# Im2col on one core: two input loads instead of three, and a first store timed by copies instead of a wait

## The chip, the cores and the metric

The kernel runs on one core of a Trainium2 chip. The metric is the device time of one execution in microseconds (us). The median of the four runs shown is 91.89 us.

## The reference

The input `x` has the shape (16, 64, 32, 32) in float32, the window is 3 x 3. Every window position becomes a column:

```python
cols = np.zeros((batch, c * kernel_size * kernel_size, h_out * w_out), dtype=np.float32)
for i in range(h_out):
    for j in range(w_out):
        patch = x[b, :, i:i + kernel_size, j:j + kernel_size]
        cols[b, :, col_idx] = patch.ravel()
```

With `h_out = w_out = 30`, one image channel (32 x 32) becomes nine planes of 30 x 30 = 900 numbers, one for each offset (ki, kj) in the window. Nothing is calculated. 4.19 MB are read and 33.18 MB are written.

## The kernel before

The 16 x 64 = 1024 channels are spread over the 128 partitions, eight neighbouring channels on each (`CPP = 8`). A partition's input is then 8 x 1024 numbers, 32 KB in one piece; its output is 8 x 9 x 900 numbers, 259.2 KB in one piece.

The whole input stays in SBUF, in `in_tile`. Three loads (L39 to L42) fill it, cut by rows of 32 numbers. The first takes rows 0 to 32, which is channel 0, 4 KB per partition. The second (`bulk`) takes rows 32 to 200, 21 KB. The third takes the rest, 7 KB. All are issued by SP. The end of `tile_im2col_kernel` moves the first load ahead of the program's opening barrier, so that it is issued as the first instruction of the span.

The loop over `c` (L47) takes two channels at a time. Each turn gets an `out_tile` of 2 x 9 planes from a pool of two buffers, so the third turn waits until the first turn's stores have landed, and the fourth until the second's has. A plane is one copy (L55 on ScalarE, ACT; L57 on VectorE, DVE) that reads a shifted 30 x 30 window of the channel and writes 900 numbers in a row. The list `on_act` deals the copies out in a fixed pattern of five, two to ACT and three to DVE. Of channel 0's nine planes ACT gets four and DVE five.

The stores go out on SP too (L60 and L75). In the first turn each channel has a store of its own of 32400 bytes per partition, since it can start earlier; the other three turns store both channels at once, 64800 bytes per partition. The order is written by hand (`manual_schedule`): each engine does its work in program order, and SP issues its DMAs one after the other, each when what it waits for is done. So SP's order is three loads, two stores of one channel, three stores of two channels.

A dependency added by hand (L66) makes the first store wait for the second load as well, though the store does not need its data.

Of the kernel before, what the change touches and what calls it, by code (L numbers as in the profile page):

```python
# [1 line left out]

# [3 lines left out]


def _im2col(ctx, tc, x, K, out):


    nc = tc.nc
    P = nc.NUM_PARTITIONS

    B, C, H, W = x.shape
    HO = H - K + 1
    WO = W - K + 1
    KK = K * K
    assert out.shape == (B, C * KK, HO * WO)
    CPP = B * C // P
    assert CPP * P == B * C and C % CPP == 0 and CPP % 4 == 0  # L20

    x_v = x.rearrange("b (cp c2) h w -> (b cp) (c2 h w)", c2=CPP)
    out_v = out.rearrange("b (cp c2 kk) n -> (b cp) c2 (kk n)", c2=CPP, kk=KK)

    in_pool = ctx.enter_context(tc.tile_pool(name="in_pool", bufs=1))
    out_pool = ctx.enter_context(tc.tile_pool(name="out_pool", bufs=2))

    ctx.enter_context(tc.manual_schedule())

    in_tile = in_pool.tile([P, CPP, H, W], x.dtype, name="in_tile")  # L30
    in_flat = in_tile.rearrange("p c h w -> p (c h w)")

    def load(queue, r0, r1):

        return queue.dma_start(
            out=in_flat[:, r0 * W : r1 * W], in_=x_v[:, r0 * W : r1 * W]
        )

    cuts = [0, H, 200, CPP * H]  # L39
    first = load(nc.sync, cuts[0], cuts[1])  # L40
    bulk = load(nc.sync, cuts[1], cuts[2])
    load(nc.sync, cuts[2], cuts[3])  # L42


    on_act = (False, True, False, True, False)
    n = 0
    for c in range(0, CPP, 2):  # L47
        out_tile = out_pool.tile([P, 2, KK, HO, WO], x.dtype, name="out_tile")
        for s in range(2):
            for kk in range(KK):  # L50
                ki, kj = divmod(kk, K)
                src = in_tile[:, c + s, ki : ki + HO, kj : kj + WO]
                dst = out_tile[:, s, kk]
                if on_act[n % len(on_act)]:
                    nc.scalar.copy(out=dst, in_=src)  # L55
                else:
                    nc.vector.tensor_copy(out=dst, in_=src)  # L57
                n += 1
            if c == 0:
                st = nc.sync.dma_start(  # L60
                    out=out_v[:, s],
                    in_=out_tile[:, s].rearrange("p kk i j -> p (kk i j)"),
                )
                if s == 0:

                    tc.add_manual_dep(  # L66
                        st.ins,
                        bulk.ins.name,
                        mybir.DependencyInfo(
                            mybir.DependencyClass.Sync, mybir.DependencyReason.DATA  # L70
                        ),
                        reason="the store follows the bulk of the loads",
                    )
        if c > 0:
            nc.sync.dma_start(  # L75
                out=out_v[:, c : c + 2].rearrange("p c n -> p (c n)"),
                in_=out_tile.rearrange("p c kk i j -> p (c kk i j)"),
            )
    return first


def kernel(
    tc: tile.TileContext,
    x: bass.AP,
    kernel_size: bass.AP,
    out: bass.AP,
):
    with ExitStack() as ctx:
        first = _im2col(ctx, tc, x, int(kernel_size), out)


    tc.close()
    tc.compile()  # L93
    blocks = tc.nc.main_func.blocks
    load = first.ins
    home = next(b for b in blocks if any(i.name == load.name for i in b.instructions))
    home.instructions = [i for i in home.instructions if i.name != load.name]
    head = list(blocks[0].instructions)
    at = next(
        k  # L100
        for k, i in enumerate(head)
        if i.engine == load.engine and type(i).__name__ == "InstDrain"
    )
    head.insert(at, load)
    blocks[0].instructions = head


# [1 line left out]
_INS = ['x', 'kernel_size']  # L109
_OUTS = [((16, 576, 900), 'float32')]  # L110

_NUMBERS = {'kernel_size': 3}


# [26 lines left out]
```

## Time and profile before

| | before |
|---|---|
| runs shown | 91.76, 91.54, 92.19, 92.02 us |
| median | 91.89 us |
| profiled execution, its time | 92.38 us |
| profiled execution, its span | 90.60 us |
| bytes read and written | 4.19 MB, 33.18 MB |
| copies on DVE | 43, of 625 ns |
| copies on ACT | 29, of 939 ns |
| DMAs, all issued by SP | 3 loads, 5 stores |

The profile is of one execution. The span goes from its first to its last instruction; 1.78 us of its time lie outside. Times in the profile count from the span's start. "SPq" is the sequencer of SP, which only waits and issues DMAs. A DMA "lands" when its semaphore shows at the waiting side that the data is there. The copies overlap a little on their engine, so a row of several copies is shorter than their number times the duration of one.

A DMA over 128 partitions is cut into 128 packets, one for each partition's piece, eight for each of the sixteen DMA engines. The trace holds a record of every packet (start, length, bytes), but not which of the sixteen engines ran it; since an engine's packets follow each other closely, the records can be sorted into sixteen chains.

### The profile page before, as it was taken

What the parts mean: (1) busy time and instruction counts of PE and PEld (TensorE: products, weight loads), DVE (VectorE), ACT (ScalarE), POOL (GpSimd) and SP (SyncE); (2) the same over time, 40 slices, a digit from 0 to 9 for tenths busy, and PEclk for the clock granted to TensorE, in tenths of its full rate; (3) what the DMA queues carried; (4) which work ended last, traced back from release to release, by engine and by line L of the source; (5) the groups of instructions that cost most, each with busy time, mean ns of one, the idle gap of its engine ahead of it and who ended that gap; (6) DMA issues with size and microseconds to landing.
All of it is one profiled execution on the core that took longest, in us unless ns stands there. A gap on an engine that the chain in (4) does not pass through costs nothing.

```text
span 90.6 us, 140 instructions
## 1 busy us (share of the span) xinstructions
DVE 23.5 (26%) x43; ACT 26.2 (29%) x30; POOL 0.2 (0%) x4
## 2 busy tenths in 40 slices
DVE  0380199980000069700000299400000000000000
ACT  5391199950000069930000299400000000000000
POOL 0000000000000000000000000000000000000000
DMA  5999999997999999973999999999999999994690
GB/s 123 460 408 446 373 485 458 458 401 300 458 458 443 672 458 458 458 343 143 458 458 458 458 458 458 458 458 458 458 458 458 429 458 458 458 458 200 286 458 0
DMA packets 1152, 37.37 MB, mean 412 GB/s; under 512 B 128, under 2 KB 128, under 8 KB 384
## 3 DMA queue, kind: packets, MB, share of 16 engines
q1 hardware_dynamic: 1152, 37.37, 96.5%
HBM read 4.19 MB, written 33.18 MB: 412 GB/s over the span
## 4 chain that ended last, share of the span: by engine, by line
DMA 46%; DVE 16%; DVEq 1%; issue 0%; SPq 0%
DMA out_dram<-out_tile 35%; DVE out_tile L57 16%; DMA in_tile<-in_x_dram 11%; DVEq L93 1%; DVEq L57 0%; SPq L75 0%
## 5 line engine op out<-in xcount | busy, mean ns | idle before, releaser
L55 ACT COPY out_tile<-in_tile 128x900 f32<-128x900 f32 x29 | 24.9, 939 | 30.7 <-DMA out_dram<-out_tile 25.3
L57 DVE COPY out_tile<-in_tile 128x900 f32<-128x900 f32 x43 | 23.5, 625 | 34.1 <-DMA out_dram<-out_tile 26.0
L55 ACT ACT_TABLE_LOAD x1 | 1.3, 1283 | 0.8 <-PEq L122 0.8
L122 POOL MEMSET const-bfloat16-1.0<- 128x1 bf16 x1 | 0.1, 101 | 0.0
L122 POOL MEMSET const-uint8-127<- 128x1 uint8 x1 | 0.1, 101 | 0.0
L122 POOL MEMSET const-float32-0.0<- 128x1 f32 x1 | 0.1, 98 | 0.2 <-issue 0.2
L122 POOL MEMSET const-float32-1.0<- 128x1 f32 x1 | 0.1, 98 | 0.0
## 6 DMA issues: line engine op xcount, KB each, us to landing
out_dram<-out_tile SPq DMA_DIRECT2D x3, 8100.0 KB, 31.3
out_dram<-out_tile SPq DMA_DIRECT2D x2, 4050.0 KB, 14.9
in_tile<-in_x_dram SPq DMA_DIRECT2D x1, 2688.0 KB, 10.1
in_tile<-in_x_dram SPq DMA_DIRECT2D x1, 896.0 KB, 11.9
in_tile<-in_x_dram SPq DMA_DIRECT2D x1, 512.0 KB, 3.7
```

The source lines that it names most:

```text
L55: nc.scalar.copy(out=dst, in_=src)
L57: nc.vector.tensor_copy(out=dst, in_=src)
L93: tc.compile()
L122: nc = _bacc.Bacc("TRN2", target_bir_lowering=False, num_devices=1)
```

## The change

The input comes in two loads: rows 0 to 64 (channels 0 and 1, 8 KB per partition) and all the rest (24 KB per partition). The first is the one that is moved ahead of the barrier.

The dependency of the first store on the second load is gone. The store now waits for channel 0's nine copies alone. Six of these (all with `kk % 3 != 1`) are on ACT instead of four, and three on DVE instead of five. All other planes are dealt out as before, so that ACT has 31 copies in all and DVE 41. Stores, tiles and the order on each engine are the same.

```diff
-    cuts = [0, H, 200, CPP * H]
-    first = load(nc.sync, cuts[0], cuts[1])
-    bulk = load(nc.sync, cuts[1], cuts[2])
-    load(nc.sync, cuts[2], cuts[3])
+    first = load(nc.sync, 0, 2 * H)
+    load(nc.sync, 2 * H, CPP * H)
...
-                if on_act[n % len(on_act)]:
+                if kk % 3 != 1 if c + s == 0 else on_act[n % len(on_act)]:
                     nc.scalar.copy(out=dst, in_=src)
...
-                st = nc.sync.dma_start(
+                nc.sync.dma_start(
                     out=out_v[:, s],
                     in_=out_tile[:, s].rearrange("p kk i j -> p (kk i j)"),
                 )
-                if s == 0:
-
-                    tc.add_manual_dep(
-                        st.ins,
-                        bulk.ins.name,
...
-                        reason="the store follows the bulk of the loads",
-                    )
```

More of the change, by code (lines that the diff above doesn't have):

```diff
@@ L63, in _im2col @@
                 )
-                if s == 0:
-                    tc.add_manual_dep(
-                        st.ins,
-                        bulk.ins.name,
-                        mybir.DependencyInfo(
-                            mybir.DependencyClass.Sync, mybir.DependencyReason.DATA
-                        ),
-                        reason="the store follows the bulk of the loads",
-                    )
         if c > 0:
```

## The prediction

> **What bounds the kernel now.** I read the page first: engine shares, the forty slices, the DMA queue.
>
> ```profile
> span 90.6 us, 140 instructions
> ...
> DVE 23.5 (26%) x43; ACT 26.2 (29%) x30; POOL 0.2 (0%) x4
> ...
> DMA  5999999997999999973999999999999999994690
> GB/s 123 460 408 446 373 485 458 458 401 300 458 458 443 672 458 458 458 343 143 458 458 458 458 458 458 458 458 458 458 458 458 429 458 458 458 458 200 286 458 0
> ...
> q1 hardware_dynamic: 1152, 37.37, 96.5%
> ```
>
> Both copying engines are three quarters idle; one DMA queue fills 96.5% of sixteen engines' span. Next the issues and their times to landing, as the DMA view gives them in narrow windows, in issue order (issue times from the timeline: 0.00, 0.80, 1.19, 10.97, 14.30, 20.21, 39.33, 57.71).
>
> ```profile
> in_tile<-in_x_dram SPq DMA_DIRECT2D x1, 512.0 KB, 3.7
> in_tile<-in_x_dram SPq DMA_DIRECT2D x1, 2688.0 KB, 10.1
> in_tile<-in_x_dram SPq DMA_DIRECT2D x1, 896.0 KB, 11.9
> ```
> ```profile
> out_dram<-out_tile SPq DMA_DIRECT2D x1, 4050.0 KB, 11.8
> ```
> ```profile
> out_dram<-out_tile SPq DMA_DIRECT2D x1, 4050.0 KB, 18.1
> ```
> ```profile
> out_dram<-out_tile SPq DMA_DIRECT2D x1, 8100.0 KB, 31.3
> ```
> ```profile
> out_dram<-out_tile SPq DMA_DIRECT2D x1, 8100.0 KB, 32.1
> ```
>
> Issue plus landing gives: last load 13.1, stores 22.8, 32.4, 51.5, 70.6, 89.8 us. The steps between are 9.7, 9.6, 19.1, 19.1 and 19.2 us for stores of 4.15, 4.15 and three times 8.29 MB, so 430 to 434 GB/s throughout. The stores run back to back; the time is 13.1 us of loading, 76.7 us of storing, and 0.8 us to the span's end. Only the first part can change. At the stores' rate 4.19 MB of loads would take 9.7 us, so 3.4 us there is not transfer.
>
> For those 3.4 us I sorted the trace's packet records into sixteen chains, each packet beginning where another ended. First packets start at 1.02 to 1.42 us and take 0.39 to 0.89 us, where later packets of that size take 0.159. Fifteen chains then run without a break and end their loads between 11.40 and 11.89. The sixteenth had finished its share of the first load earliest, at 2.744; its next packet begins 0.68 us later, at 3.425, and lasts 1.51 us where its kind takes 0.80. That chain needs 10.02 us from there to its last load, against about 8.61 for a chain without the stall: 1.41 us lost. It ends its loads at 12.76, and goes on without a gap to 89.29. The other fifteen end at 88.53 to 88.68. So one stalled chain sets this execution's end.
>
> Last, the waits and the timeline around the first store:
>
> ```profile
> SPq L60 <- DMA in_tile<-in_x_dram: 9.3, 1, 9.3
> ```
> ```profile
> 3.69 3.48 ACT L55 COPY out_tile<-in_tile 128x900 f32<-128x900 f32 x4 [1.61 <-DMA in_tile<-in_x_dram]
> 3.69 2.78 DVE L57 COPY out_tile<-in_tile 128x900 f32<-128x900 f32 x5 [3.69 <-DMA in_tile<-in_x_dram]
> 10.90 8.54 ACT L55 COPY out_tile<-in_tile 128x900 f32<-128x900 f32 x10 [3.73 <-DMA in_tile<-in_x_dram]
> 10.90 9.23 DVE L57 COPY out_tile<-in_tile 128x900 f32<-128x900 f32 x17 [4.43 <-DMA in_tile<-in_x_dram]
> 10.97 3.67 SPq L60 DMA_DIRECT2D out_dram<-out_tile  x2
> ```
>
> Channel 0 is copied by 7.17, yet SP holds its store until the second load has landed. Issued at 10.97, its packets begin at 11.83 to 11.96, or 0.86 us after the issue: by then fifteen chains have been empty for 0.01 to 0.57 us. Only the stalled chain loses nothing by it.
>
> **The change, part by part.**
>
> *One load fewer.* A chain's eight packets follow each other every 155.3, 795.4 and 268.3 ns for 4096, 21504 and 7168 bytes: 4.7 ns each plus 0.0368 ns per byte. By that line 8192 bytes take 306 and 24576 take 908. Now 8 x (155.3 + 795.4 + 268.3) = 9.75 us; then 8 x (306 + 908) = 9.71. That is on the path: minus 0.04, minus 0.05 with the semaphore packet that goes. A DMA issue on SP (0.33 to 0.42 us) goes too, at a time when SP only waits.
>
> The Trainium skill, "DMA: Bandwidth & Descriptors", section "Anatomy of one DMA", puts a fixed cost of about 2.0 us on each DMA (fitted on GpSimd's path), which would make this edit worth minus 2.0 us. The row shows 6 ns between one load's last packet and the next load's first.
>
> *The first load twice as large.* It lands later, by 8 x (306 - 155) = 1.21 us: at 3.69 + 1.21 = 4.90. Lower bound 3.69 (nothing added), upper 7.4 (the whole time to landing doubles). I take 4.90, since start-up is paid once per chain and the spacing is measured. DVE and ACT begin 1.2 us later, which only the first store can feel.
>
> *The stall.* What made that chain wait is not in the trace. Its shape is that of a chain that ran dry: the earliest to finish, a gap, then a packet with 0.71 us too much, like the 0.24 to 0.74 us too much of the very first packets. If its part of the second load was ready at 3.42, a first load that lasts until 3.95 or later on every chain (2.744 + 1.21) covers it. Bounds: minus 1.41 us on this chain, or nothing; above nothing if it strikes a chain without this one's lead, which ended its first load 0.57 us ahead of the last. I take the cover, because the packet began late; a slow read alone would have made it long, not late.
>
> *Six planes on ACT, no hold.* Four copies take 3.48 us and ten 8.54, so each further one 0.843; six take 3.48 + 2 x 0.843 = 5.17. DVE's three end long before. Channel 0 is ready at 4.90 + 5.17 = 10.07, SP issues 0.03 later (as after ACT's last copy at 39.30, issued 39.33), at 10.10, and packets are ready 0.86 later, at 10.96. The chains end loading at 11.35 to 11.84 (today's less 0.05). So the store is in time by 0.4 us, the gaps of 0.01 to 0.57 close, and the load packets hide the issue: while the same store was issued at 10.97, load packets kept their 0.272 us. Bounds with landing at 3.69 and 7.4: packets at 9.75, or 13.46, 1.6 us too late for the last chain. Behind the store on SP is the second one, which is ready later anyway.
>
> *What follows.* Channel 1 no longer waits for the second load. ACT does nine copies, 3.48 + 5 x 0.843 = 7.70, to 12.6; the second store is issued then instead of at 14.30, while the first runs until after 21. The next tile needs the 24 KB load, landed at about 12.1 instead of 10.9; ACT's seven copies (6.01 us in the fourth tile) end at 18.6, issue near 18.7 against 20.21, and the queue needs it at 31.1. Nothing there reaches the path; its cover is 12 us of queued stores. After that order and counts are the same.
>
> The Trainium skill's "Perfetto Trace Analysis", section "DMA Optimizations", says that smaller pieces let work start sooner where DMA engines are idle; that speaks against merging the loads. Here the copies' later start is 1.2 us, hidden as shown; by the rule alone it would be plus 1.2.
>
> **The sum, in the profiled execution.** Without a stall the last chain leaves its loads at 11.84, and stores take 76.5 (the stalled chain) to 76.8 us (the others): end 88.3 to 88.6, taken as 88.5, against 89.29, so minus 0.8. Its time of 92.38 (span 90.60, 1.78 around it) becomes 91.6. The median shown, 91.89, is 0.49 lower. If all runs had the full stall they come to 91.1. If the runs differ by the stall, a stall-free one today ends at 88.68, which is 92.38 - 0.61 = 91.77, about that of the two fastest (91.54, 91.76); from those the closed gaps take 0.18 (88.68 to 88.5): 91.4 to 91.6. I take 91.4, between the two readings; this case by itself spans 91.0 to 91.7.
>
> **Rivals.**
>
> *The stall stays as it is.* It may be a slow stretch of memory, met by any second load. Then only 0.05 us goes: 91.84, between 91.5 and 92.2. For it: the runs shown spread by 0.65 us, so it may come and go. Against: the late start.
>
> *The stall strikes a chain without a lead: slower.* Place: the first 24 KB packet of a chain that leaves the first load last. It would end its loads at 11.84 + 1.41 = 13.25 instead of 12.76: plus 0.49 on the profiled time, 92.87; on the median 92.4 if all runs stall today, more if they don't; I put it at 92.6. If the median's 0.49 is a shorter stall, its last chain leaves the loads at 12.27, and this decides from 0.9 us of stall on the last chain (11.84 + 0.9 = 12.27 + 0.46). For it: nothing ties the stall to that chain. Against: it did strike the one that was ahead.
>
> *The store comes too late.* If the first load lands after 5.78, 5.78 + 5.17 + 0.03 + 0.86 = 11.84 and all chains run dry. At the bound of 7.4 stores begin at 13.46 and end at 90.1: plus 0.9, 92.8 by the median. Against: it takes 0.9 us more than the spacing gives.
>
> **How the numbers follow.** The covered stall: 0.55, of which 0.40 beyond 0.5% (below 91.43) and 0.15 within. The unchanged stall: 0.22, of which 0.19 within and 0.03 above 92.35. The worse stall: 0.18, slower. The late store: 0.05, of which 0.02 within. So faster 0.40, same 0.36, slower 0.24; 0.5%, 0.46 us, is about what a measurement of this kernel can tell from no change. The range, 91.0 to 92.4, leaves out some 0.08 below and 0.12 above.
>
> **What would show it.** Right: a first landing near 4.9, the first store issued near 10.1, a 24 KB landing near 12.1, no chain idle between loads and store, the first store landing near 21.8 instead of 22.8, the span near 89.7. Wrong: a load landing at 13 or later (a stall), the first store issued after 10.9, or steps between store landings that are no longer 9.6 and 19.1.

## The result, and the profile after

The changed kernel takes 91.45 us (median of 53 runs, 91.25 to 91.69); the kernel before, beside it, 91.64 us (78 runs, 91.37 to 93.78). The ratio is 0.9971, with a 95% interval of 0.9962 to 0.998. So it is 0.3% faster: clear of chance, but within the 0.5% that the prediction called no change. The forecast time was 91.4, and the result lies inside its range. What changed more than the middle is the upper end: 15 of the 78 runs before lie above 92.0 us, and none of the 53 after above 91.69. The means differ by 0.31 us (91.77 and 91.45), and about half of that is this upper end: the other 63 runs of before have a mean of 91.62.

The page of the changed kernel answers the lines of before: the queue, and the load issues.

```profile
span 89.6 us, 136 instructions
...
DMA  5989899999889999995799999999999998489990
...
q1 hardware_dynamic: 1008, 37.37, 97.2%
...
in_tile<-in_x_dram SPq DMA_DIRECT2D x1, 3072.0 KB, 11.4
in_tile<-in_x_dram SPq DMA_DIRECT2D x1, 1024.0 KB, 4.9
```

The first store's time from issue to landing, from the DMA view between 9.5 and 11 us:

```profile
out_dram<-out_tile SPq DMA_DIRECT2D x1, 4050.0 KB, 11.7
```

Its timeline up to the second store (start, length, engine, line, count; in brackets the idle time before and what ended it):

```profile
4.88 13.60 ACT L54 COPY out_tile<-in_tile 128x900 f32<-128x900 f32 x16 [2.82 <-DMA in_tile<-in_x_dram]
4.88 4.93 DVE L56 COPY out_tile<-in_tile 128x900 f32<-128x900 f32 x9 [4.88 <-DMA in_tile<-in_x_dram]
10.07 2.87 SPq L59 DMA_DIRECT2D out_dram<-out_tile  x2
12.19 6.01 DVE L56 COPY out_tile<-in_tile 128x900 f32<-128x900 f32 x11 [2.37 <-DMA in_tile<-in_x_dram]
```

The first load lands at 4.86 (4.90 was forecast), and the first store is issued at 10.07 (10.10) and lands at 21.8 (21.8). The wait on a load that held SP for 9.3 us is gone; SP now waits for the copies:

```profile
SPq L59 <- ACT out_tile L54: 5.5, 2, 3.4
SPq L59 <- DVE out_tile L56: 5.5, 1, 5.5
```

In the packet records, sorted into sixteen chains as before, the chains end their loads between 11.14 and 11.73 and begin the store within 0.01 us. No chain stalls, and none is empty. Stores end at 88.32, and the span is 89.6 (89.7).

So far everything is as forecast, except for the execution it was compared with. A second and a third trace of the kernel before were taken:

> The kernel before, unchanged, for a second trace. If the stall of one chain is a rare event, this trace shows none: the second load then lands near 10.0 instead of 10.88, the held store is issued near 10.1, its packets come near 11.0, no chain is empty, and the span is near 89.7. If the stall comes every time, it is there again and the span is 90 or more.

Measured: 91.60 us, span 89.8. The timeline of this second trace, and its second and third load:

```profile
3.71 3.47 ACT L55 COPY out_tile<-in_tile 128x900 f32<-128x900 f32 x4 [1.64 <-DMA in_tile<-in_x_dram]
...
10.10 4.32 ACT L55 COPY out_tile<-in_tile 128x900 f32<-128x900 f32 x5 [2.92 <-DMA in_tile<-in_x_dram]
10.10 4.39 DVE L57 COPY out_tile<-in_tile 128x900 f32<-128x900 f32 x8 [3.61 <-DMA in_tile<-in_x_dram]
10.16 3.67 SPq L60 DMA_DIRECT2D out_dram<-out_tile  x2
```
```profile
in_tile<-in_x_dram SPq DMA_DIRECT2D x1, 2688.0 KB, 9.3
in_tile<-in_x_dram SPq DMA_DIRECT2D x1, 896.0 KB, 11.1
```

The second load is seen at 10.10 instead of 10.90, and the held store goes out at 10.16 instead of 10.97, nearly where the changed kernel's does (10.07). Its packets meet the end of the loads (11.38 to 11.89) without a gap.

> The same kernel once more, for a third trace, with the same expectation as the second.

Measured: 91.64 us, span 89.9, store issued at 10.26, again no stall. The execution on which the prediction was built, 92.38 us, was thus one of the minority above 92.0. In the common execution, as these two traces show it, the hold and the six planes put the store at nearly the same place.

### The profile page after: what moved, and what is told of

It is laid out like the page before. It is cut to its first block, busy times and chain, and to the rows that moved or that the text cites. A ratio compares the mean times of both kernels' runs of the same rounds, so it can differ in the third digit from the quotient of the medians.

```text
span 89.6 us, 136 instructions
## 1 busy us (share of the span) xinstructions
DVE 22.4 (25%) x41; ACT 27.7 (31%) x32; POOL 0.2 (0%) x4
## 4 chain that ended last, share of the span: by engine, by line
DMA 41%; ACT 15%; DVE 6%; DVEq 1%; issue 0%
DMA out_dram<-out_tile 36%; ACT out_tile L54 15%; DVE out_tile L56 6%; DMA in_tile<-in_x_dram 5%; DVEq L82 1%; DVEq L56 0%
## 5 line engine op out<-in xcount | busy, mean ns | idle before, releaser
L54 ACT COPY out_tile<-in_tile 128x900 f32<-128x900 f32 x31 | 26.5, 940 | 28.2 <-DMA out_dram<-out_tile 25.4
L56 DVE COPY out_tile<-in_tile 128x900 f32<-128x900 f32 x41 | 22.4, 625 | 34.3 <-DMA out_dram<-out_tile 27.0
## 6 DMA issues: line engine op xcount, KB each, us to landing
in_tile<-in_x_dram SPq DMA_DIRECT2D x1, 3072.0 KB, 11.4
```

## The experiments

Times are medians; beside each stands the median of the kernel before, run together with it. The experiments fall into three such groups, each on another chip (1 to 4; 5 to 8; 9, 10 and the two further traces), and the share of before's runs above 92.0 us differs between them: 3 of 17, 1 of 29, 7 of 17. Comparisons across groups go by the ratios to before or by the traces; where medians are compared directly, the text says so.

**1. The hold taken out, nothing else.**

```diff
-                if s == 0:
-
-                    tc.add_manual_dep(
-                        st.ins,
-                        bulk.ins.name,
...
-                        reason="the store follows the bulk of the loads",
-                    )
```

> The kernel before with the first store's wait on the second load taken out and nothing else. Theory A (a chain that stalls after a short first load sets the slow executions): the loads are unchanged, so the stalls stay, and the time stays that of before within 0.15 us, with single executions still above 92.0 us. Theory B (the held store is what costs): without the hold the store is issued near 7.2 us, no chain runs empty, and the time falls to that of the changed kernel, 0.2 us below before.

Measured: 92.78 us (5 runs) beside 91.62, ratio 1.0115 (1.0086 to 1.0145). Both theories fall: the kernel gets slower by 1.1 us (1.16 by the medians, 1.05 by the ratio). The store is issued early, and the last load lands late:

```profile
7.05 6.67 SPq L60 DMA_DIRECT2D out_dram<-out_tile  x2
```
```profile
in_tile<-in_x_dram SPq DMA_DIRECT2D x1, 896.0 KB, 12.1
```

That load was issued at about 1.2, so it lands at 13.3; in the second trace of before it takes 11.1 from the same issue. In the packet records its 7168-byte packets last 431 ns on average instead of 272. Eight on each chain make 1.27 us.

**2. The changed kernel with the old dealing, so with an early store.**

```diff
-                if kk % 3 != 1 if c + s == 0 else on_act[n % len(on_act)]:
+                if on_act[n % len(on_act)]:
```

> The changed kernel with the old dealing of channel 0 (five planes on DVE, four on ACT), so that its store is issued near 8.4 us instead of 10.07. Theory A: the store only waits in the queue behind the loads, so the time is that of the changed kernel within 0.1 us. Theory C (a store issued early, among the loads, disturbs them, and six planes on ACT are needed to time it): slower than the changed kernel by 0.2 us or more, with load packets longer than their 309 and 912 ns after the issue.

Measured: 92.46 us (6 runs) beside 91.62, ratio 1.008 (1.0051 to 1.0109). The time and the load packets are as theory C has them. The timeline shows the store at 8.35, and the next turn's copies waiting for the 24 KB load until 13.07, where the changed kernel has them at 12.19:

```profile
8.35 2.92 SPq L59 DMA_DIRECT2D out_dram<-out_tile  x2
13.07 1.79 ACT L54 COPY out_tile<-in_tile 128x900 f32<-128x900 f32 x2 [2.21 <-DMA in_tile<-in_x_dram]
13.07 1.17 DVE L56 COPY out_tile<-in_tile 128x900 f32<-128x900 f32 x2 [2.22 <-DMA in_tile<-in_x_dram]
```
```profile
in_tile<-in_x_dram SPq DMA_DIRECT2D x1, 3072.0 KB, 12.3
```

In the records the 24 KB packets that start between 4.3 and 9.2 last 912 ns. Those that start from 9.25 to 10 last 0.13 to 0.23 us longer on average, the last ones, from 10.25, 0.6 to 0.73 us longer. The sum is 0.87 us on each chain.

**3. Loads of 4 and 28 KB.**

```diff
-    first = load(nc.sync, 0, 2 * H)
-    load(nc.sync, 2 * H, CPP * H)
+    first = load(nc.sync, 0, H)
+    load(nc.sync, H, CPP * H)
```

> The changed kernel with loads of 4 and 28 KB per partition. Six planes of channel 0 on ACT, no hold, store issued near 8.9 us. Theory A: the short first load is back, so a chain may run empty before its part of the second load is there; executions above 92.0 us come back, about 2 in 10, and the median is about that of before. Theory D (it is the third load and its extra packets that cost): no such executions, median as the changed kernel's.

Measured: 92.14 us (12 runs) beside 91.62, ratio 1.0063 (1.0033 to 1.0093). The median misses both expectations, and experiment 2 says why: the store is issued at 8.74, and the last 28 KB packet of each chain lasts about 0.55 us longer.

```profile
8.74 7.62 SPq L59 DMA_DIRECT2D out_dram<-out_tile  x2
```

The spread is as theory A has it: three of the twelve runs stand at 92.58, 93.28 and 93.63, the other nine between 91.92 and 92.18. The trace is of a run of 91.93, so that a chain stalled in the three high ones is inferred, not seen.

**4. Eight planes on ACT: a late store.**

```diff
-                if kk % 3 != 1 if c + s == 0 else on_act[n % len(on_act)]:
+                if kk != 4 if c + s == 0 else on_act[n % len(on_act)]:
```

> The changed kernel with eight of channel 0's planes on ACT instead of six: channel 0 is ready 2 x 0.843 = 1.69 us later, the store issued at 11.76, packets from 12.62. All chains, which end their loads between 11.14 and 11.73 in the changed kernel, run empty for 0.9 to 1.5 us; the last chain sets the end, so slower than the changed kernel by 0.9 us (1.0 at the highest, if all chains start together and the slowest in storing counts). If the queue did not run empty, or the sixteen engines made it up later, no change.

Measured: 92.43 us (6 runs) beside 91.62, ratio 1.0076 (1.0051 to 1.0102), so about 0.95 us above the changed kernel, as expected. The store is issued at 11.64; the chains end their loads at 11.24 to 11.67, the first store packet comes at 12.49.

```profile
11.64 2.88 SPq L59 DMA_DIRECT2D out_dram<-out_tile  x2
```

**5. Three loads with a first one of 8 KB, and the hold.**

```diff
-    cuts = [0, H, 200, CPP * H]
+    cuts = [0, 2 * H, 200, CPP * H]
```

> The kernel before with its first load raised from 4 to 8 KB per partition and its second cut to 17 KB; still three loads, hold and dealing as before. Theory A (a first load of 4 KB lets a chain run empty): no execution above 92.0 us, median 91.5 to 91.6. Rival D (it is the third load or the hold): the slow executions of before, about 2 in 10 above 92.0, stay.

Measured: 91.53 us (12 runs, 91.46 to 91.73) beside 91.53, ratio 1.000 (0.999 to 1.001). As theory A expects, no run lies above 92.0, though the third load and the hold are there. But of the 29 runs of before beside it only one did, so twelve runs without one are weak evidence against rival D; the weight lies on experiments 3 and 7, which have neither the third load nor the hold and keep the high times. The hold released the store at 10.11:

```profile
10.11 1.00 SPq L60 DMA_DIRECT2D out_dram<-out_tile  x2
```

**6. The early store on another queue.** The kernel of experiment 2 with its first store issued by ACT.

```diff
-                nc.sync.dma_start(
+                (nc.scalar if s == 0 else nc.sync).dma_start(
```

> The changed kernel with the old dealing of channel 0 and its store issued by ACT, on ACT's own DMA queue, near 8.4 us. Theory E (load packets become long when a store's packets are queued behind them in the same queue): from its arrival near 9.2 us the store's packets take turns with the loads' on each chain, load packets keep 912 ns, no chain is empty, and the time is that of the changed kernel within 0.15 us. Theory F (loads and stores disturb each other in memory whatever the queue): the load packets after 9.2 us are long again, by 0.6 us or more, and the time is 0.5 us or more above the changed kernel's.

Measured: 92.25 us (6 runs) beside 91.53, ratio 1.0075 (1.0059 to 1.0091). Theory E falls: another queue saves little or nothing (0.95 us above the changed kernel by the ratios, where experiment 2 has 1.0). The size is that of theory F; that the two disturb each other in memory is not shown by it.

```profile
8.33 0.37 ACTq L59 DMA_DIRECT2D out_dram<-out_tile  x1
```
```profile
out_dram<-out_tile ACTq DMA_DIRECT2D x1, 4050.0 KB, 22.7
...
in_tile<-in_x_dram SPq DMA_DIRECT2D x1, 3072.0 KB, 12.1
```

The 24 KB load takes 12.1 us to land, against 11.4. Its packets are longer by 0.75 us on each chain, again only the last two. The Trainium skill ("DMA: Bandwidth & Descriptors", section "Queues, rings and completion order") has each DMA engine take turns between its queues, packet by packet, where its packet is a group of typically 9 to 17 descriptors (orders to move one piece each); whether that is one packet of this trace's records, no run here shows. Here no store packet is recorded before 11.83, when the first chain was done with its loads, 3.5 us after the store's issue on its own queue. Turns show later, between the two stores: from 14.97 to 16.85 us on, each chain runs one packet of each in turn, and this store lands at 31.0, where the first store of the changed kernel lands at 21.8. The turns begin late, too: after the second store's packets could have come (issue at 11.40 plus 0.85), two or three packets of the first still start on each chain. When the first store's could have come (8.33 plus 0.85), just two load packets per chain were left to start. So the absence of turns among the loads does not speak against the page.

**7. 4 and 28 KB again, with the store at the right time.** As experiment 3, with seven planes on ACT (`kk % 4 != 1`).

> Loads of 4 and 28 KB per partition, seven of channel 0's planes on ACT, so that the store is issued at 3.56 + 6.01 + 0.03 = 9.60 and its packets come at 10.46, when nearly all chains have begun their last load packet (10.0 to 10.6). Theory A (short first load lets a chain run empty) with theory E (the store's time decides the rest): most executions near the changed kernel's, 91.5 to 91.6, but some above 92.0 us. Theory E alone: all within 0.2 us of the changed kernel's.

Measured: 91.40 us (12 runs) beside 91.53, ratio 0.9997 (0.9976 to 1.0017). Eight runs lie between 91.28 and 91.46, four at 91.71, 91.94, 92.04 and 92.17. "Theory E" here and in experiment 8 stands for the store's time as what decides the rest, not for the shared queue. Both halves of theory A with E's timing come out. The store goes out at 9.64 and lengthens nothing; high times are back with the short first load, though again no trace fell on one.

```profile
9.64 0.35 SPq L59 DMA_DIRECT2D out_dram<-out_tile  x1
```

**8. Five planes on ACT.** Channel 0's dealing with `kk % 2 == 0`.

> The changed kernel with five of channel 0's planes on ACT instead of six: the store is issued at 4.88 + 4.32 + 0.03 = 9.23, its packets come at 10.09, before every chain's last load packet starts (10.2 to 10.8). Theory E: that one packet on each chain becomes longer by about 0.6 us, as with loads of 4 and 28 KB, so 0.5 to 0.7 us slower than the changed kernel, near 92.0. If the early store costs by the time it is early (1.0 us for 1.72 us early), 0.84 us early costs 0.5: 91.95; the packets tell the two apart, since by the second the excess would be spread.

Measured: 91.70 us (12 runs, 91.62 to 91.77) beside 91.53, ratio 1.0013 (1.0001 to 1.0025). The direction is right, the size half of what was expected: about 0.25 us above the changed kernel by medians, 0.4 by the ratios. The store is issued at 9.03; the last 24 KB packet of fourteen chains is longer, by 0.34 us on average over the sixteen, and no other packet after the issue is. So it is one packet, not a spread excess, as theory E had it, but at little more than half the size.

```profile
9.03 2.88 SPq L59 DMA_DIRECT2D out_dram<-out_tile  x2
```

**9. Seven planes on ACT.** Dealing with `kk % 4 != 1`.

> The changed kernel with seven of channel 0's planes on ACT: the store is issued at 4.88 + 6.01 + 0.03 = 10.92, its packets come at 11.78, after all chains have ended their loads (11.1 to 11.7). The last chain sets the end: 0.05 to 0.2 us slower than the changed kernel, 91.5 to 91.65, a third of the step that five planes or eight planes make.

Measured: 91.59 us (12 runs, 91.51 to 91.73) beside 91.90, ratio 0.9972 (0.9947 to 0.9997). By medians this is in the range expected; by the ratio it equals the changed kernel. Nine of the 17 runs of before beside it lay at 91.9 or above, so the ratio can't decide. In the trace the store is issued at 10.85, its first packet comes at 11.70, and the loads are over at 11.26 to 11.73, so most chains are empty for a while. The span is 89.8 instead of 89.6, but the changed kernel's own runs spread from 89.5 to 89.9.

```profile
10.85 2.87 SPq L59 DMA_DIRECT2D out_dram<-out_tile  x2
```

**10. A first load of 2 KB.**

```diff
-    first = load(nc.sync, 0, 2 * H)
+    first = load(nc.sync, 0, H // 2)
+    load(nc.sync, H // 2, 2 * H)
```

> The changed kernel with its first load of 8 KB cut into 2 and 6 KB (three loads, no hold, six planes). Channel 0 is there when the 6 KB have landed, near 4.9, so the store is issued near 10.1 as in the changed kernel. Theory A (a short first load lets a chain run empty before its part of the next is there): the first load's packets end near 2.2 us, earlier than in the kernel before, so slow executions come back, 2 in 10 or more at 0.4 us or more over the median. Without theory A: as narrow as the changed kernel, 91.4 to 91.7.

Measured: 92.73 us (6 runs, 92.34 to 94.29) beside 91.90, ratio 1.0113 (1.0066 to 1.016). The profiled execution is the slowest of the six, 94.29. One chain ends its 6 KB packets at 6.67, the other fifteen between 4.18 and 4.75; it also ends its loads at 13.94, the others by 12.03. So one chain again lost about 2 us between a short first load and the next. Two of the six runs stand more than 0.4 us above the median (93.57, 94.29), as theory A has it. The test is not a clean one: with two loads to wait for, ACT's table load stands behind the wait, which delays the store by another 1.28 us in the traced run, and presumably in all six, since the instructions are the same. There it was issued at 13.54, when fifteen chains were empty already.

```profile
7.06 1.28 ACT L55 ACT_TABLE_LOAD   x1 [7.06 <-DMA in_tile<-in_x_dram]
7.08 4.93 DVE L57 COPY out_tile<-in_tile 128x900 f32<-128x900 f32 x9 [7.08 <-DMA in_tile<-in_x_dram]
8.35 6.01 ACT L55 COPY out_tile<-in_tile 128x900 f32<-128x900 f32 x7
13.54 0.35 SPq L60 DMA_DIRECT2D out_dram<-out_tile  x1
```

The first store by its time of issue, with the packet records' answer:

| kernel | store issued | load packets longer, per chain | first store packet after the first chain's loads | span |
|---|---|---|---|---|
| 1, no hold | 7.05 | 1.27 us | at once | 91.0 |
| 6, on ACT's queue | 8.33 | 0.75 us | at once | 90.5 |
| 2, old dealing | 8.35 | 0.87 us | at once | 90.8 |
| 3, 4 and 28 KB | 8.74 | 0.58 us | at once | 90.2 |
| 8, five planes | 9.03 | 0.36 us | at once | 89.9 |
| 7, 4 and 28 KB, seven planes | 9.64 | 0.06 us, all before the issue | at once | 89.6 |
| changed kernel | 10.07 | 0.01 us | at once | 89.6 |
| 9, seven planes | 10.85 | 0 | 0.44 us | 89.8 |
| 4, eight planes | 11.64 | 0 | 1.25 us | 90.6 |

## Why the prediction was right, and where its steps were not

**What bounds the kernel** held: in every run the stores follow each other without a break, and the differences arise before the first of them.

**The times of the change** held: landing 4.86, issue 10.07, no gap. The way a late store was priced, by the wait of the last chain, came out roughly where experiment 4 made it late: 0.95 us for a first packet at 12.49, after the last load at 11.67.

**One load fewer**, minus 0.05 us: the nearest measure is the changed kernel against experiment 5, which has three loads, a first load of 8 KB and a store issued at 10.11: 91.45 and 91.53, with ratios 0.9971 and 1.000. That is 0.08 us by the medians and 0.27 by the ratios, but the two ratios stand on a before with 15 of 78 and with 1 of 29 runs above 92.0. The traces say it better: with two loads and no lengthened packets (the changed kernel, experiments 4, 7 and 9) the last chain ends its loads at 11.67 to 11.75, with three loads and no stall (experiment 5 and the two further traces of before) at 11.87 to 11.96. The averages lie 0.18 us apart, and 0.14 over all sixteen chains. So the term was too small by some 0.1 us. The fixed 2.0 us for each DMA that the Trainium skill gives for GpSimd's path ("DMA: Bandwidth & Descriptors", section "Anatomy of one DMA") is not what a queued load cost here.

**The stall** was the mis-sized term. The sum took 0.8 us off one profiled execution and placed the outcome between two readings of the median. The two further traces show no stall, so the median hardly holds it. In its place the median gained 0.2 us, about what the earlier end of two loads gives: the last chain's stores begin at 11.73 instead of 11.89 and 11.96. Of that 0.05 is the packet count; the two further traces of before have second-load packets some 15 ns longer on average, 0.12 us on a chain of eight, and why is open. Experiments 5 and 7 point the same way: the first load of 8 KB with three loads and the hold left the median at before's 91.53, and two loads without the hold, with 4 KB first, brought it to 91.40. The number came out at 91.4 because the sum was anchored at the two lowest times shown in the end, not because the step was right; that closeness is luck. One reading of the trace was not exact either: besides the stall, one of the other fifteen chains had a break of 0.18 us near 5.3, which did not set the end.

That a longer first load ends the stalls is supported: with a first load of 8 KB, 107 runs (53, and 54 of experiments 2, 4, 5, 6, 8 and 9) hold none more than 0.25 us above its kernel's median, while with 4 KB it was 15 of 78, and 3 of 12 in experiment 3 as in 7, that stood at least 0.38 us above theirs. A stall of one chain is seen in the two traces that fell on such a run (92.38 and 94.29); for the others it is inferred from the time. Why a chain's next packets come late, and whether it is the bytes or the time of the first load that counts, stays open. Experiment 1, also with 4 KB, had none in 5 runs.

**Closed gaps**, minus 0.18: there were none to close in the common execution, since the hold is released by the second load itself, and with no stall that comes at 10.1.

**An early issue costs nothing** was wrong. The prediction gave packets at 9.75, an issue at 8.89, no price, and named only a store that comes late; experiment 8, issued at 9.03, cost 0.25 to 0.4 us. The row it leaned on, load packets that kept their 0.272 us after the issue at 10.97, ended within 1.8 us of that issue. Experiments 1, 2, 3, 6 and 8 show the mirror of that rival: a store issued at 9.03 or before lengthens the load packets still to come, by 0.36 to 1.27 us on each chain. So the hold was not idle caution, and taking it out alone is a loss of 1.1 us; the six planes are what pays for it. Their window is narrow: in the changed kernel 10.07 showed no cost, 9.03 did, and at 10.85 chains ran empty, though the time did not settle a cost. With other loads, 9.64 (experiment 7) and 10.16 and 10.26 (the two further traces of before) showed none.

Lined up on the store's issue, the records of experiments 1, 2, 3, 6 and 8 agree on one thing: no load packet that was due to end within 1.5 us after the issue was longer by more than 0.01 us, and the first longer ones were due to end 1.5 to 2.4 us after it. In the changed kernel the last load packet ends 1.66 us after the issue, in experiment 7 2.1 us.

What makes the packets longer was not settled. A shared queue is not needed for it (experiment 6). In experiment 1 the 21 KB packets that started between 8.0 and 8.9 kept their 0.80 us, although a store issued at 7.05 could have been there at 7.9; only the 7 KB packets behind them grew, and of these the ones that started after 12.0 were nearly back at their length (309 ns on average). So neither the time since the issue nor the place in the chain gives the rule by itself.

## What to carry to other kernels

In a kernel bound by DMA like this one, the change from loading to storing is a place of its own: here a store issued too early made the loads in flight longer, one issued too late left the engines empty, and both cost about 1 us for 1.6 to 1.7 us. Look for its moment by counting the copies or the bytes ahead of it, and check it in the packet records. Before a sum is built on one trace, take a second: the stall that this one showed goes with times that came in one run of five.

## What the runs showed of the hardware that was not expected

- The last 24 KB load packet of each chain lasted 1.2 to 1.8 us instead of 0.91 where a store was waiting, on the same queue or on another (experiments 2 and 6).
- A store's packets, issued on ACT's queue at 8.33, began on each chain only after that chain's loads (the first at 11.83).
- After a first load of 2 or 4 KB per partition, one chain of sixteen lost about 2 and 1.4 us around the start of the next load, in two traced executions.
- The table load of ACT stood behind the wait of the first copy when that copy waited for two loads (experiment 10: 7.06 instead of 0.78 us in the changed kernel).
